# Encoder block on one core: where the opening builds the differences of its transposed input

## The chip, the cores and the metric

The kernel runs on one core of one Trainium2 chip. Five engines of the core run side by side, each with an instruction stream of its own that it works through in order: TensorE (PE in the profile; its weight loads are a row of their own, PEld), VectorE (DVE), ScalarE (ACT), GpSimd (POOL) and SyncE (SP), which here issues most DMAs. PE writes its products to PSUM, eight banks of 128 x 512 float32; DVE and ACT read them there. The metric is the device time of one execution in microseconds (us), as a median of runs.

## The reference: what is computed

A transformer-like block over 1024 tokens of width 1024, float32, one layer. The opening, which is all that this change touches, is the first two of these lines: the layer norm of the input, and the projection of its result by one matrix of 1024 x 11776.

```python
h = layer_norm(x, ln_in_g, ln_in_b)
proj = h @ w_in[l]
aq, ak, av, hq, hf_fwd, hf_bwd, hi, hg, ga, gh = jnp.split(proj, split_idx, axis=-1)
att = dilated_attention(aq, ak, av, slopes)
rec = hgrn2(hq, hf_fwd, hf_bwd, hi, hg, lower_bounds[:, l], hgrn_norm_g[l])
merged = jax.nn.sigmoid(ga) * (att @ w_att_up[l]) + jax.nn.sigmoid(gh) * (rec @ w_hgrn_up[l])
h = layer_norm(DEEPNORM_ALPHA * h + merged @ w_o[l], ln1_g[l], ln1_b[l])
gate, up = jnp.split(h @ w_ffn_in[l], 2, axis=-1)
h = layer_norm(DEEPNORM_ALPHA * h + (jax.nn.silu(gate) * up) @ w_ffn_out[l], ln2_g[l], ln2_b[l])
```

## The kernel before

**Products.** Every large matrix product is done by the Strassen-Winograd scheme: both factors are cut into 2 x 2 blocks, and seven block products replace eight. Each float32 block is further split into a high part (rounded to the type `float32r`, by ACT) and a low part (the rest, by DVE or POOL), and a block product sums high x high, high x low and low x high in PSUM (`mm3`, L270 to L272). A block product of 512 x 512 moving data takes 4 x 3 = 12 instructions of PE, called products below.

**The moving side.** `phase0` (L316) makes it from x. Token rows come in eight tiles `xt` of 128 x 1024. For each, `stats` (DVE, then three small steps on POOL) finds mean and inverse deviation, and `norm(tt, q)` normalises half q of tile tt (512 columns) on ACT. `turn` transposes 128 x 128 pieces on PE into PSUM banks (tag `sd`, four of them, shared with some block products). The four blocks of the transposed input are b11 and b21 (first and second 512 features of tiles 0 to 3), b12 and b22 (the same of tiles 4 to 7). The gain of the layer norm is a factor and its bias a summand per partition in this layout. From the blocks come t1 = b12 - b11, t2 = b22 - t1, t3 = b22 - b12 and t4 = b21 - t2, each in four pieces k of 128 features.

Helpers of `phase0`: `scaled` takes a bank times the gain to SBUF, on ACT or DVE; `less` takes a bank times the gain less another tile (DVE); `hi` makes a high part with the bias (ACT); `lo` makes the low part (DVE). Tiles that are needed only in the opening are lent the buffers of later forms (`lent`): w11 (b11 without its bias) lies in that of b22's high part, t1 in that of t3's, w22 (b22 without its bias) in that of t4's, z2 (t2 without its bias) in that of t4's low part. `forms(n)` gives a buffer its final use, which waits until what was lent is read. w21 is b21 without its bias; its buffers are named v in the profile.

Before, t3's difference is made in SBUF by POOL, z2 - w11 (L467), t4's too, w21 - z2 (L482); b22 is copied raw from its banks by ACT and split late, after t3.

**The stationary side.** `stream` (L615) is a generator; each `next` (by `run` in `phase0`) issues one block product. Its order is: product 1 (b11) for two units of two column groups each, product 2 (b21) for both, then products 6 (t2), 5 (t1), 7 (t3), 3 (b22), 4 (t4) of unit 0, then of unit 1, and so on over 23 units. Ahead of each, `sums` (L644) forms the sums of weight blocks and `prep` splits a weight block into `w_hi` (ACT, L212) and `w_lo` (POOL, L222) and issues the DMA that refills the block. `leave` evicts the banks into the outputs of the projection (DVE and ACT, L529 to L559, and L680) at high priority.

**Order.** The program's text gives priorities. At build a scheduler lays out each engine's stream from them by its own estimate of time; `ordered`, `left` and `behind` add order edges between two instructions. Loads of x and of weights are kept in program order on SP's queue (`queued`).

Of the kernel before, what the change touches and what calls it, by code (L numbers as in the profile page):

```python
# [10 lines left out]
F32 = mybir.dt.float32  # L11
F32R = mybir.dt.float32r
I32 = mybir.dt.int32
AF = mybir.ActivationFunctionType
# [65 lines left out]
class Block:  # L80
# [152 lines left out]
        self.issued[key] = ins.ins.name  # L233
        return ins

    gone = None

    def left(self, ins):
        self.gone = ins.ins.name
# [76 lines left out]
    def phase0(self, pool, work):  # L316
# [4 lines left out]
        def lent(tag):  # L321
            t = self.xp.tile([128, 4, HALF], F32, name=f"lent_{tag}", tag=tag, bufs=1)
            return [t[:, k, :] for k in range(4)]

        w11, t1, w22, z2 = (lent(z) for z in ("xb22hi", "xt3hi", "xt4hi", "xt4lo"))
        w21 = [self.half("v21") for _ in range(4)]

        strict = True

        def act(*args, **kw):  # L330
            ins = nc.scalar.activation(*args, **kw)
            return self.ordered("xact", ins) if strict else ins

        def dve(ins):
            return self.ordered("xdve", ins) if strict else ins
# [9 lines left out]
        def stats(tt):  # L345
            st = self.tiny.tile([128, 2, 6], F32, name="bn0", tag="bnst", bufs=3)
            for j in range(2):
                dve(nc.vector.bn_stats(st[:, j, :], xs[tt][:, HALF * j:HALF * (j + 1)]))
            mv = self.mv0[:, tt, :]
            dve(nc.vector.bn_aggr(mv[:, 0:2], st))  # L350
            nc.gpsimd.tensor_scalar(mv[:, 2:3], mv[:, 1:2], LN_EPS, None, op0=OP.add)
            nc.gpsimd.tensor_tensor(mv[:, 2:3], mv[:, 2:3], self.mhalf[:, 0:1], OP.pow)
            nc.gpsimd.tensor_scalar(mv[:, 3:4], mv[:, 0:1], mv[:, 2:3], -1.0, op0=OP.mult, op1=OP.mult)

        def norm(tt, q):
            x, mv = xs[tt][:, HALF * q:HALF * (q + 1)], self.mv0[:, tt, :]
            return act(x, x, AF.Identity, bias=mv[:, 3:4], scale=mv[:, 2:3])

        def turn(tt, q, ks=range(4)):
# [7 lines left out]
        def column(n, k):  # L367
            return self.col[n][:, k:k + 1]

        def scaled(w, k, q, on_act):  # L370

            g = column("gin", 4 * q + k)
            if on_act:
                act(w[k], banks[k], AF.Copy, scale=g)
            else:
                dve(nc.vector.tensor_scalar(w[k], banks[k], g, None, op0=OP.mult))

        def less(o, k, q, w):

            dve(nc.vector.scalar_tensor_tensor(o[k], banks[k], column("gin", 4 * q + k), w[k], op0=OP.mult,  # L380
                                               op1=OP.subtract))

        def hi(name, k, src, b=None):
            z = self.xb[name][0][:, k, :]
# [23 lines left out]
        for tt in range(4):  # L408
            norm(tt, 0)
            turn(tt, 0)  # L410
            if tt < 3:
                stats(tt + 1)
                norm(tt, 1)
        bias = [[column("bin", 4 * q + k) for k in range(4)] for q in range(2)]
        scaled(w11, 0, 0, True)
        scaled(w11, 1, 0, False)
        scaled(w11, 3, 0, False)
# [20 lines left out]
            self.left(lo("b21", k, w21, bias[1][k]))  # L438
        self.rest()
        strict = False  # L440
        for tt in range(4, 8):
            norm(tt, 0)
            if tt < 7:
                stats(tt + 1)
            norm(tt, 1)
        run(3)
        for k in (0, 2):
            for tt in range(4, 8):
                turn(tt, 0, (k, k + 1))
            for i in (k, k + 1):  # L450
                less(t1, i, 0, w11)
            run()
        for k in (0, 2):
            for tt in range(4, 8):
                turn(tt, 1, (k, k + 1))
            for i in (k, k + 1):
                less(z2, i, 1, t1)
            for i in (k, k + 1):
                h = hi("t2", i, z2, bias[1][i]), lo("t2", i, z2, bias[1][i])
                scaled(w22, i, 1, True)  # L460
            run()
        for k in range(4):
            self.behind(hi("t1", k, t1), h[0].ins.name)
            last = lo("t1", k, t1)
            self.behind(last, h[1].ins.name)
        for k in range(4):
            self.behind(nc.gpsimd.tensor_sub(w11[k], z2[k], w11[k]), last.ins.name)  # L467
        diff = self.tiny.tile([128, 4], F32, name="diff", tag="bnmv", bufs=3)
        nc.gpsimd.tensor_sub(diff, self.col["bin"][:, 4:8], self.col["bin"][:, 0:4])
        run(2)  # L470
        self.forms("t3")
        for k in range(4):
            hi("t3", k, w11, diff[:, k:k + 1])
            last = lo("t3", k, w11, diff[:, k:k + 1])
        run(2)
        self.forms("b22")
        for k in range(4):
            hi("b22", k, w22, bias[1][k])
            lo("b22", k, w22, bias[1][k])
        run()  # L480
        for k in range(4):
            self.behind(nc.gpsimd.tensor_sub(w21[k], w21[k], z2[k]), last.ins.name)  # L482
        self.forms("t4")
        for k in range(4):
            hi("t4", k, w21)
# [129 lines left out]
    def stream(self, tiles, pool):  # L615


        nc, tc = self.nc, self.tc
        self.cols = [c for c, _ in tiles]
        O = self.ORDER  # L620
        order = [(n, (p,)) for p in O[:2] for n in (0, 1)]
        order += [(n, O[2:] if n < 2 else O) for n in range(len(tiles) // 4)]
        seq = [(n, g, p) for n, part in order for p in part for g in range(2)]
        after = {6: "a11", 7: "a21", 3: "a12", 4: "a22"}
        A, first = [{}, {}], {}
        for g in range(2):
            A[g]["a11"] = self.block(0, g, "a11")
        yield
        for g in range(2):
            first[g, 1] = self.block(1, g, "a11", pool)  # L630
        for g in range(2):
            A[g]["a12"] = self.block(0, g, "a12")
        yield
        for b in ("a21", "a22"):
            for g in range(2):
                A[g][b] = self.block(0, g, b)
        yield
        state = [[{}, {}], [{}, {}]]
        ready = {}

        def early(n):
            return tc.high_priority(offset=self.evac_ahead if n > 1 else 0)

        def sums(i):  # L644
            if i >= len(seq):
                return
            n, g, p = seq[i]
            a = A[g]
            with early(n):
                if p == 6:  # L650
                    a["s1"] = self.blk.tile([128, 4, 128], F32, name="ws1", tag=f"s1{g}", bufs=1)
                    self.behind(nc.vector.tensor_add(a["s1"], a["a21"], a["a22"]))
                    nc.vector.tensor_sub(a["a11"], a["s1"], a["a11"])  # L653
                    nc.gpsimd.tensor_sub(a["a21"], a["a22"], a["a11"])  # L654
                    a["s3"], a["s2"] = a["a21"], a["a11"]
                elif p == 3:
                    self.behind(nc.vector.tensor_sub(a["a12"], a["a12"], a["s2"]))
                    a["s4"] = a["a12"]

        def prep(i):  # L660
            if i >= len(seq):
                return
            n, g, p = seq[i]
            if n == 1 and p == 2:
                first[g, 2] = self.block(1, g, "a12", pool)
            with early(n):
                ready[i] = self.granules()
                self.split(*ready[i], first[g, p] if n == 1 and p < 3 else A[g][self.PRODUCTS[p][0]],
                           key="w" if i < 4 else None)
            if p in after and 4 * n + 4 < len(tiles):  # L670
                A[g][after[p]] = self.block(n + 1, g, after[p])

        def bank(n, g, p):
            if (n, p) in ((0, 5), (0, 2), (1, 2)):
                return self.ps_sd()
            return self.ps_pj(2 * g + (n + (p == 1)) % 2)

        def keep(ps, tag):
            t = self.ws.tile([128, HALF], F32, name="wkeep", tag=tag, bufs=1)
            nc.scalar.copy(t, ps)  # L680
            return t

        for i in range(3):
            prep(i)
        yield
        for i, (n, g, p) in enumerate(seq):
            late = i + 5 < len(seq) and seq[i + 5][0::2] == (1, 6)
            if not late:
                sums(i + 5)
            prep(i + 3)  # L690
            if late:
                sums(i + 5)
            s = state[n % 2][g]
            if p in (1, 2) or p == 5 and n < 2:
                s[min(p, 2)] = bank(n, g, p)
            ps = s[1 if p in (1, 6, 7, 4) else 2]
            hi, lo = ready.pop(i)
            xhi, xlo = self.xb[self.PRODUCTS[p][1]]
            for k in range(4):
                self.mm3(ps, hi[:, k, :], lo[:, k, :], xhi[:, k, :], xlo[:, k, :], p in (1, 2, 5) and k == 0, k == 3,  # L700
                         skip_group_check=True)
            self.leave(tiles[4 * n + 2 * g:4 * n + 2 * g + 2], p, ps, s, keep,
                       f"k{5 if (n, p) == (1, 1) else 1}{g}", f"k5{g}")
            yield 4 * n + 2 * g + 2 if p == 4 else 0
# [1208 lines left out]
```

## Time and profile before

| | us |
|---|---|
| median of 3 runs | 2074.36 |
| lowest and highest | 2071.59, 2077.41 |
| profiled execution, its own time | 2071.3 |
| its span | 2069.5 |

| engine, whole span | busy us |
|---|---|
| PE | 2016.2 |
| DVE | 1325.4 |
| POOL | 1074.7 |
| ACT | 953.8 |

The profile lists instructions with start and duration, and groups of them. The idle time ahead of an instruction and the one that released it stand in brackets or behind the last bar. Names are those of the program's tiles: `sd` and `pj` are PSUM banks, `wa`, `wfirst` and `ws` weight blocks and their sums, `lent_...` the buffers lent in the opening, `vc` the columns of gains and biases, `evh` and `wkeep` evicted results. A matmul's duration overlaps that of the next. The granted clock is 1.00 at full speed and 0.50 at half.

### The profile page before, as it was taken

The numbers are of one execution on the slowest core, as the hardware profiler recorded it, in microseconds if no ns is written. First come the engines' busy times: TensorE is split into PE (matmuls) and PEld (weight loads), VectorE is DVE, ScalarE is ACT, GpSimd is POOL, SyncE is SP. The second block draws the span as 40 slices with busy tenths as digits, with TensorE's granted clock in tenths as the row PEclk, the third lists the DMA queues.
The fourth block names the chain that finished last, engine by engine and source line by source line (L and its number), as shares of the span: only waits on it lengthen the run. The fifth ranks groups of instructions, "written<-read, shape, count | busy, mean of one in ns | idle before, by whom it ended". The sixth has DMA issues, their size and how long they took to land. (4 is left out here: it accounts for less than half of the span.)

```text
span 2069.5 us, 30921 instructions
## 1 busy us (share of the span) xinstructions
PE 2016.2 (97%) x10974; PEld 1669.0 (81%) x10974; DVE 1325.4 (64%) x2017; ACT 953.8 (46%) x1968; POOL 1074.7 (52%) x919
## 2 busy tenths in 40 slices
PE   7899999999999999999999999999999999999998
PEld 5688888888887888888888888787888888888876
DVE  6966645884368744776343225547776776758777
ACT  6554455553655436454365432244433333334542
POOL 5766744776356653665536662344665665620012
PEclk9999999999999999999999999999999999999999
DMA  5443433435333452344524376444444443447423
GB/s 157 133 139 125 158 122 105 157 126 173 97 123 133 131 163 93 122 139 137 166 93 154 124 249 219 154 145 139 154 137 138 133 137 132 144 158 270 164 89 127
DMA packets 274844, 297.95 MB, mean 144 GB/s; under 512 B 14017, under 2 KB 207362, under 8 KB 274690
## 3 DMA queue, kind: packets, MB, share of 16 engines
q1 hardware_dynamic: 268384, 274.78, 41.0%
q10 hardware_dynamic: 6306, 21.20, 2.6%
q8 instruction: 86, 1.41, 0.3%
q14 instruction: 68, 0.56, 0.1%
HBM read 201.29 MB, written 94.63 MB: 143 GB/s over the span
## 5 line engine op out<-in xcount | busy, mean ns | idle before, releaser
L222 POOL TENSOR_TENSOR w_lo<-wa,w_hi 128x512 fp32r<-128x512 f32 x272 | 363.2, 1345 | 277.8 <-ACT w_hi L212 250.3
L212 ACT CAST w_hi<-wa 128x512 fp32r<-128x512 f32 x272 | 168.4, 620 | 251.0 <-PE pj L271 165.3
L222 POOL TENSOR_TENSOR w_lo<-wsum,w_hi 128x512 fp32r<-128x512 f32 x88 | 127.7, 1460 | 111.3 <-PE sd L272 60.7
L222 POOL TENSOR_TENSOR w_lo<-f_raw,w_hi 128x512 fp32r<-128x512 f32 x66 | 102.1, 1555 | 55.2 <-ACT w_hi L212 54.0
L208 POOL TENSOR_TENSOR mv<-mv,mhalf 128x1 f32<-128x1 f32 x16 | 10.8, 680 | 208.3 <-DVE mv L207 208.2
L212 ACT CAST w_hi<-wsum 128x512 fp32r<-128x512 f32 x88 | 54.7, 621 | 122.2 <-PE sd L271 118.7
L270 PE MATMUL pj<-xt1hi,w_hi 128*128 128x512 f32 x252 | 99.8, 396 | 3.6 <-DVE evh L531 1.9
L270 PE MATMUL pj<-xb22hi,w_hi 128*128 128x512 f32 x252 | 99.3, 394 | 0.0
L272 PE MATMUL pj<-xb22hi,w_lo 128*128 128x512 f32 x252 | 98.5, 392 | 0.4 <-POOL w_lo L222 0.3
L542 DVE TENSOR_TENSOR evh<-wkeep,pj 128x512 f32<-128x512 f32 x45 | 30.8, 684 | 106.4 <-PE pj L272 61.2
L271 PE MATMUL pj<-xb22lo,w_hi 128*128 128x512 f32 x252 | 98.5, 391 | 0.0
L272 PE MATMUL pj<-xt1hi,w_lo 128*128 128x512 f32 x252 | 98.5, 391 | 0.0
L271 PE MATMUL pj<-xt1lo,w_hi 128*128 128x512 f32 x252 | 98.3, 390 | 0.0
L212 ACT CAST gwsum<-a_raw 128x512 fp32r<-128x512 f32 (+1 forms) x78 | 47.7, 616 | 101.6 <-PE pj L271 47.2
L654 POOL TENSOR_TENSOR wa<-wa,wa 128x512 f32<-128x512 f32 x46 | 65.1, 1424 | 49.5 <-DVE wa L653 44.0
L680 ACT COPY wkeep<-pj 128x512 f32<-128x512 f32 x136 | 79.4, 584 | 21.6 <-DVE evh L558 11.9
L531 DVE TENSOR_TENSOR evh<-wkeep,pj 128x512 f32<-128x512 f32 x66 | 57.5, 879 | 44.5 <-PE pj L272 33.9
L222 POOL TENSOR_TENSOR w_lo<-ws,w_hi 128x512 fp32r<-128x512 f32 x46 | 63.2, 1378 | 43.1 <-ACT w_hi L212 42.9
L222 DVE TENSOR_TENSOR gwkeep<-a_raw,gwsum 128x512 fp32r<-128x512 f32 (+1 forms) x78 | 57.7, 739 | 42.0 <-ACT gwsum L212 39.1
L270 PE MATMUL pj<-xt4hi,w_hi 128*128 128x512 f32 x192 | 76.4, 398 | 3.5 <-DVE evh L531 2.4
L272 PE MATMUL pj<-xt2hi,w_lo 128*128 128x512 f32 x192 | 75.5, 394 | 3.7 <-POOL w_lo L222 3.7
L270 PE MATMUL pj<-xb11hi,w_hi 128*128 128x512 f32 x192 | 76.8, 402 | 1.3 <-DVE wkeep L556 1.3
(421 smaller groups left out, 6585.1 us busy)
## 6 DMA issues: line engine op xcount, KB each, us to landing
wa<-in_w_in_dram SPq DMA_DIRECT2D x184, 256.0 KB, 3.3
f_raw<-in_w_ffn_in_dram SPq DMA_DIRECT2D x44, 512.0 KB, 4.0
a_raw<-gd SPq DMA_DIRECT2D x30, 512.0 KB, 3.6
gd<-fc SPq DMA_DIRECT2D x44, 256.0 KB, 2.0
gd<-fs SPq DMA_DIRECT2D x33, 256.0 KB, 2.1
tg<-evh SPq DMA_DIRECT2D x32, 256.0 KB, 2.3
tg<-tg SPq DMA_DIRECT2D x16, 512.0 KB, 3.6
y<-ahs SPq DMA_DIRECT2D x16, 512.0 KB, 4.6
```

Of the source, the lines that this page charges most:

```text
L208: nc.gpsimd.tensor_tensor(mv[:, 2:3], mv[:, 2:3], self.mhalf[:, 0:1], OP.pow)
L212: ins = nc.scalar.copy(hi, src) if eng_hi == "act" else nc.vector.tensor_copy(hi, src)
L222: ins = e.tensor_sub(lo, src, hi.bitcast(F32))
L270: nc.tensor.matmul(ps, whi, xhi, start=first, stop=False, **kw)
L271: nc.tensor.matmul(ps, whi, xlo, start=False, stop=False, **kw)
L272: self.product = nc.tensor.matmul(ps, wlo, xhi, start=False, stop=last, **kw).ins.name
L531: self.left(nc.vector.tensor_tensor(o, self.order_src(add, g, kind), s, OP.add))
L542: self.left(nc.vector.tensor_add(t, add, ps))
L654: nc.gpsimd.tensor_sub(a["a21"], a["a22"], a["a11"])
L680: nc.scalar.copy(t, ps)
```

## The change

It has five parts, all in `phase0` and `sums`:

- the first halves of the last two row tiles (tt 6 and 7) are normalised on DVE, the other 14 halves stay on ACT; the statistics of tiles 5 to 7 come first, then all first halves of tiles 4 to 7, then all second halves;
- the raw b12 is kept: `scaled` on ACT writes w12 from the bank (four instructions), and once the bank of b22 is there, `less` on DVE turns it into t3's difference in place (four). POOL's four subtractions for t3 go;
- b22's parts are made while its banks are held: the high part by ACT from the bank, then the high part less the bias (hb) by ACT with a negated bias column (nbin, one small POOL instruction), then the low part by DVE as bank times gain less hb. The four raw copies and the later split of b22 go;
- t4's four differences move from POOL to DVE;
- the first weight sums (product 6, first group) are held back in `later` and issued behind the first two pieces of t1. The three products that follow t3's split are asked for in one go instead of two and one.

```diff
-        w11, t1, w22, z2 = (lent(z) for z in ("xb22hi", "xt3hi", "xt4hi", "xt4lo"))
+        w11, w12, t1, hb, z2 = (lent(z) for z in ("xb22hi", "xt4hi", "xt3hi", "xt3lo", "xt4lo"))
...
             x, mv = xs[tt][:, HALF * q:HALF * (q + 1)], self.mv0[:, tt, :]
+            if tt > 5 and q == 0:
+                return dve(nc.vector.tensor_scalar(x, x, mv[:, 2:3], mv[:, 3:4], op0=OP.mult, op1=OP.add))
             return act(x, x, AF.Identity, bias=mv[:, 3:4], scale=mv[:, 2:3])
...
+        nc.gpsimd.tensor_scalar(nbin, self.col["bin"][:, 4:8], -1.0, None, op0=OP.mult)
...
-        for tt in range(4, 8):
-            norm(tt, 0)
-            if tt < 7:
-                stats(tt + 1)
-            norm(tt, 1)
+        for tt in range(5, 8):
+            stats(tt)
+        for q in range(2):
+            for tt in range(4, 8):
+                norm(tt, q)
+        self.later = []
         run(3)
         for k in (0, 2):
             for tt in range(4, 8):
                 turn(tt, 0, (k, k + 1))
             for i in (k, k + 1):
-                less(t1, i, 0, w11)
+                scaled(w12, i, 0, True)
+                self.left(less(t1, i, 0, w11))
+            if k == 0:
+                for z in self.later:
+                    z()
+                self.later = None
             run()
+        self.forms("b22")
         for k in (0, 2):
             for tt in range(4, 8):
                 turn(tt, 1, (k, k + 1))
             for i in (k, k + 1):
                 less(z2, i, 1, t1)
             for i in (k, k + 1):
+                less(w12, i, 1, w12)
+                g, b, z = column("gin", 4 + i), bias[1][i], self.xb["b22"][0][:, i, :]
+                act(z, banks[i], AF.Identity, bias=b, scale=g)
+                act(hb[i], z.bitcast(F32), AF.Identity, bias=nbin[:, i:i + 1])
+                dve(nc.vector.scalar_tensor_tensor(self.xb["b22"][1][:, i, :], banks[i], g, hb[i], op0=OP.mult,
+                                                   op1=OP.subtract))
+            for i in (k, k + 1):
                 h = hi("t2", i, z2, bias[1][i]), lo("t2", i, z2, bias[1][i])
-                scaled(w22, i, 1, True)
             run()
...
-        for k in range(4):
-            self.behind(nc.gpsimd.tensor_sub(w11[k], z2[k], w11[k]), last.ins.name)
...
-            hi("t3", k, w11, diff[:, k:k + 1])
-            last = lo("t3", k, w11, diff[:, k:k + 1])
-        run(2)
-        self.forms("b22")
+            hi("t3", k, w12, diff[:, k:k + 1])
+            last = lo("t3", k, w12, diff[:, k:k + 1])
+        run(3)
         for k in range(4):
-            hi("b22", k, w22, bias[1][k])
-            lo("b22", k, w22, bias[1][k])
-        run()
-        for k in range(4):
-            self.behind(nc.gpsimd.tensor_sub(w21[k], w21[k], z2[k]), last.ins.name)
+            self.behind(nc.vector.tensor_sub(w21[k], w21[k], z2[k]), last.ins.name)
...
-        def sums(i):
+        def sums(i, again=False):
             if i >= len(seq):
                 return
             n, g, p = seq[i]
             a = A[g]
+            if n == 0 and p == 6 and self.later is not None and not again:
+                self.later.append(lambda: sums(i, True))
+                return
```

More of the change, by code (lines that the diff above doesn't have):

```diff
@@ L234, in ordered @@
         return ins
-    gone = None
+    gone = later = None
     def left(self, ins):
@@ L323, in lent @@
             return [t[:, k, :] for k in range(4)]
-        w11, t1, w22, z2 = (lent(z) for z in ("xb22hi", "xt3hi", "xt4hi", "xt4lo"))
+        w11, w12, t1, hb, z2 = (lent(z) for z in ("xb22hi", "xt4hi", "xt3hi", "xt3lo", "xt4lo"))
         w21 = [self.half("v21") for _ in range(4)]
         strict = True
+        nbin = self.tiny.tile([128, 4], F32, name="nbin", tag="nbin", bufs=1)
         def act(*args, **kw):
@@ L378, in less @@
         def less(o, k, q, w):
-            dve(nc.vector.scalar_tensor_tensor(o[k], banks[k], column("gin", 4 * q + k), w[k], op0=OP.mult,
-                                               op1=OP.subtract))
+            return dve(nc.vector.scalar_tensor_tensor(o[k], banks[k], column("gin", 4 * q + k), w[k], op0=OP.mult,
+                                                      op1=OP.subtract))
         def hi(name, k, src, b=None):
@@ L458, in phase0 @@
             for i in (k, k + 1):
+                less(w12, i, 1, w12)
[3 more added lines that the diff above has]
+                dve(nc.vector.scalar_tensor_tensor(self.xb["b22"][1][:, i, :], banks[i], g, hb[i], op0=OP.mult,
+                                                   op1=OP.subtract))
+            for i in (k, k + 1):
                 h = hi("t2", i, z2, bias[1][i]), lo("t2", i, z2, bias[1][i])
-                scaled(w22, i, 1, True)
             run()
```

## The prediction

> **What bounds the kernel now.** I read the page first, then the windows, then the order of time on each engine over the opening.
>
> ```profile
> span 2069.5 us, 30921 instructions
> PE 2016.2 (97%) x10974; PEld 1669.0 (81%) x10974; DVE 1325.4 (64%) x2017; ACT 953.8 (46%) x1968; POOL 1074.7 (52%) x919
> ```
> ```profile
> 0.00:100.00 100.00, 76.88 (x315) 58.51 (x316) 81.58 (x107) 60.20 (x101) 64.35 (x80) 0.95 0.47 147
> 100.00:500.00 400.00, 398.06 (x2524) 335.04 (x2523) 257.93 (x399) 203.00 (x472) 253.51 (x236) 1.00 0.42 136
> ```
>
> TensorE (PE) bounds the span. The windows (stretch, length, busy time of PE, weight loads, DVE, ACT, POOL, granted clock, DMA) put 23.1 us of its 53.3 us of idle into the first 100 us, and 1.9 us into the next 400. The change works only in those 100 us, so I ask what PE waits for there, in order of time:
>
> ```profile
> 34.59 0.55 PE L364 MATMUL sd<-tabs_sb,xt 128*128 128x128 f32 x3
> 37.16 1.15 PE L364 MATMUL sd<-tabs_sb,xt 128*128 128x128 f32 x7 [2.03 <-DVE evh L542]
> 39.13 0.79 PE L270 MATMUL sd<-xb21hi,w_hi 128*128 128x512 f32 x1 [0.82 <-DVE lent_xt3hi L380]
> 44.42 1.16 PE L364 MATMUL sd<-tabs_sb,xt 128*128 128x128 f32 x8
> 53.41 0.39 PE L272 MATMUL sd<-xb21hi,w_lo 128*128 128x512 f32 x1
> 57.26 0.39 PE L270 MATMUL sd<-xt1hi,w_hi 128*128 128x512 f32 x1
> 58.42 0.40 PE L271 MATMUL sd<-xt1lo,w_hi 128*128 128x512 f32 x1
> 61.34 0.51 PE L271 MATMUL sd<-xt1lo,w_hi 128*128 128x512 f32 x1 [2.33 <-DVE xt1lo L390]
> 65.25 0.63 PE L270 MATMUL pj<-xt3hi,w_hi 128*128 128x512 f32 x2
> 73.00 0.39 PE L272 MATMUL pj<-xt3hi,w_lo 128*128 128x512 f32 x1
> 80.15 0.50 PE L270 MATMUL pj<-xt4hi,w_hi 128*128 128x512 f32 x1 [0.82 <-ACT w_hi L212]
> 89.60 0.50 PE L272 MATMUL pj<-xt2hi,w_lo 128*128 128x512 f32 x1 [1.22 <-POOL w_lo L222]
> 96.98 0.50 PE L272 MATMUL pj<-xt2hi,w_lo 128*128 128x512 f32 x1 [2.52 <-POOL w_lo L222]
> ```
>
> The reader sees a start, a duration and, in brackets, idle time and its releaser. Products overlap, so their price is from start to start: five from 57.26 to 58.42 give 0.23 us at full speed. Four stretches fall short of that:
> - A, 34.59 to 44.42: 10 transposes (0.145 each by the row of eight) and 12 products need 4.2 us and take 9.8. Lost 5.6.
> - B, 58.42 to 65.25: nine products need 2.07 and take 6.83. Lost 4.8.
> - C, 73.00 to 80.15: fifteen products need 3.4 and take 7.15. Lost 3.7; the waits there are for b22's low part and a weight.
> - D, the two waits for weights of the second unit: 3.7.
>
> All four together are 17.8 us, the most that an opening without stalls could return. Part of A and B is clock:
>
> ```profile
> 41.26:44.67 3.41, 3.41 (x10) 2.52 (x10) 0.01 (x1) 0.40 (x1) 0.76 (x1) 0.50 0.00 0
> 61.73:65.14 3.41, 3.07 (x8) 1.97 (x7) 3.21 (x10) 1.47 (x3) 0.85 (x5) 0.50 0.89 263
> 58.32:61.73 3.41, 1.08 (x6) 0.53 (x5) 3.41 (x4) 2.30 (x5) 2.67 (x3) 1.00 0.41 121
> 92.45:95.86 3.41, 1.81 (x7) 0.86 (x5) 3.41 (x3) 1.23 (x3) 3.41 (x4) 1.00 0.87 258
> ```
>
> A stretch in which PE was busy 1.08 of 3.41 us is followed by 3.41 us at half clock; one with 1.81 is not. So a gap of 2.3 us can cost 1.7 us more. The Trainium skill (TensorE: Matmul & The Clock Gate, "Part 1: The HAM clock gate") asks for a whole idle window of about 3.4 us before the clock halves. By that rule a remaining gap under 3 us costs only itself; here the trace halved it after 2.33 us, and the trace decides.
>
> **The change part by part.**
>
> *Rows, norms and first weight sums (stretch A).* What stood ahead of t1:
>
> ```profile
> 31.74 0.27 POOL L353 TENSOR_SCALAR mv<-mv 128x1 f32<-128x1 f32 x1
> 32.86 0.75 DVE L391 SCALAR_TENSOR_TENSOR xb21lo<-v,vc,xb21hi 128x512 fp32r<-128x512 f32 x1 [1.89 <-ACT xb21hi L331]
> 33.53 2.38 DVE L652 TENSOR_TENSOR ws<-wa,wa 128x512 f32<-128x512 f32 x2
> 36.12 1.53 ACT L331 ACTIVATE xt<-xt,mv 128x512 f32<-128x512 f32 x2
> 38.34 2.71 DVE L380 SCALAR_TENSOR_TENSOR lent_xt3hi<-sd,vc,lent_xb22hi 128x512 f32<-128x512 f32 x4
> 44.66 0.69 DVE L556 TENSOR_TENSOR wkeep<-wkeep,sd 128x512 f32<-128x512 f32 x1 [3.60 <-PE sd L272]
> ```
>
> The page names the DVE eviction as releaser of the transposes at 37.16, but the last row's first half is normalised by ACT only at 36.12 to 36.9, so ACT was as late. Both go: that half moves to DVE, which was idle for 1.89 us, and its statistics are ready at 32.0; the weight sums (33.53) step behind the first two t1. A DVE normalise from SBUF has no row: at best it hides in the 1.89 us, at worst two cost 2 x 1.2 (the half of 2.38); I take 0.7 each, as for t1, hidden. ACT loses two of 0.77 and gains nothing ahead of that. Then t1's first two are done at about 35, PE's second b21 group starts near 36 instead of 39.13 and at full clock ends near 39 instead of 44.42: 5.5 us ahead. The weight sums land about 2 us later, under a product group whose own end was 44.42; if that cover fails they cost those 2 us.
>
> *More work ahead of t2.* The raw b12 is kept by ACT (four, as many as the b22 copies that go) and turned into t3's difference by DVE; b22's high part, a copy less the bias (ACT), and its low part (DVE) now come straight from the PSUM banks ahead of t2.
>
> ```profile
> L380 DVE SCALAR_TENSOR_TENSOR lent_xt4lo<-sd,vc,lent_xt3hi 128x512 f32<-128x512 f32 x4 | 2.8, 743 | 0.0
> L391 DVE SCALAR_TENSOR_TENSOR xb22lo<-lent_xt4hi,vc,xb22hi 128x512 fp32r<-128x512 f32 x4 | 5.9, 1530 | 0.0
> L390 DVE TENSOR_TENSOR xt1lo<-lent_xt3hi,xt1hi 128x512 fp32r<-128x512 f32 x4 | 5.8, 1490 | 0.0
> L467 POOL TENSOR_TENSOR lent_xb22hi<-lent_xt4lo,lent_xb22hi 128x512 f32<-128x512 f32 x4 | 6.4, 1634 | 0.0
> L482 POOL TENSOR_TENSOR v<-v,lent_xt4lo 128x512 f32<-128x512 f32 x4 | 5.5, 1405 | 0.0
> ```
> ```profile
> 52.13 3.49 DVE L391 SCALAR_TENSOR_TENSOR xt2lo<-lent_xt4lo,vc,xt2hi 128x512 fp32r<-128x512 f32 x2
> 55.54 1.77 DVE L390 TENSOR_TENSOR xt1lo<-lent_xt3hi,xt1hi 128x512 fp32r<-128x512 f32 x1
> 59.54 4.04 DVE L390 TENSOR_TENSOR xt1lo<-lent_xt3hi,xt1hi 128x512 fp32r<-128x512 f32 x3
> 70.73 1.27 DVE L1073 TENSOR_SCALAR gna<-lbm 128x16 f32<-128x16 f32 x1
> 82.60 0.68 DVE L390 TENSOR_TENSOR xt4lo<-v,xt4hi 128x512 fp32r<-128x512 f32 x1
> ```
>
> DVE's clean price is 0.7 a step (0.68 for the last t4 low part); from two SBUF operands it rises to 1.5 to 1.8 while POOL works, from PSUM it stays at 0.74. From 33.6 to the last t2 low part DVE has t1 2.7, four weight sums 2.7, five eviction steps 3.4, t2 2.8, the new t3 differences 2.8 and b22 low parts 2.8, t2 low parts 2.8: 20.0, so 53.6 clean. Before, 5.6 fewer ended at 55.6, because DVE stood idle for 3.6 us behind A and POOL's 6.4 us of t3 differences lay beside it. POOL's weight low parts remain, and the b22 low parts wait for two ACT steps each while their banks stay taken: between 0 (other DVE work fills it) and 4 x 2 x 0.77 = 6.2 us (nothing does, ACT's price from the row at 36.12); I take 1.5, near the lower end, because the next bank's t3 difference and the evictions stand ready. So t2 is whole at 55, only 0.6 us earlier. PE, 5.5 us ahead, ends b21 at 48 (53.64 before), does what it can of t2 and then waits: at the start of t1 it has about 1 us left of the 5.5.
>
> *t1 (stretch B).* POOL's 6.4 us are gone and t1's low parts follow at once: four of 0.7 to 1.5 end between 57.8 and 61, against 63.6. The 24 t1 products (24 x 0.23 = 5.5 us) end near 62; from 57.26, with B's 4.8, they ended at 67.5. Of B's 4.8 I count 4.0.
>
> *b22 and t3 (stretch C).* b22 is complete some 20 us before use and 5.9 us of contended DVE work has become 2.8. t3 needs only its splits. Of 3.7 I count 3.5, leaving the weight wait.
>
> *t4 on DVE.* Four differences: 4 x 0.68 clean, 4 x 1.5 contended, 2.7 to 6.0; I take 4. They queue behind t3's last low part; behind them stand t4's low parts and evictions. DVE's balance to the last t4 low part (83.3) is +2.8 (t3) +4 (t4) -3.1 (b22) -3.2 (the three steps from 52.13 paid 5.3 beside POOL's t3 work, 2.1 clean) -3.6 (idle before the eviction at 44.66) and -3 (three 16-column steps like the one at 70.73 paid some 1.1 too much beside POOL's t4 work): about 6 ahead, where PE is 8.5 ahead. The t4 products take 5.5 us, so the last low part may trail; I charge 1.0.
>
> *Weights of the second unit (stretch D).*
>
> ```profile
> 73.19 3.41 POOL L222 TENSOR_TENSOR w_lo<-wa,w_hi 128x512 fp32r<-128x512 f32 x2
> 80.01 1.02 SPq L249 DMA_DIRECT2D wa<-in_w_in_dram  x2
> ```
>
> POOL's 5.5 us of t4 work held the splits at 73.19, and the next weight loads went out only at 80.01. Without it they go earlier, but so does PE. No DMA is added or moved past another; the negated bias is one small POOL step (0.27, as the row at 31.74) long before its use. Between 0 and 3.7; I take 2.0.
>
> **Sum:** 1.0 + 4.0 + 3.5 - 1.0 + 2.0 = 9.5 us. The profiled execution took 2071.3 us (span 2069.5), 3.1 under the median 2074.36, so 2061.8 for it and **2065** as a median.
>
> **Rivals.**
> - *DVE sets t2, or the gap only moves to the weights of the second unit.* For it: DVE was busy 81.58 of the first 100 us already. If every step from SBUF pays POOL's price, t2 is whole at 59 to 60, the wait takes in a half clock (1.7), t1 ends where it did, and C alone is won: 3 us, 2071. If the second unit's weights come when they came, little is won: 2073. Against: C and A do not hang on t2.
> - *Slower: DVE as the bound through t4.* Its in-order queue takes 5.6 us more ahead of t2, waits for ACT in each b22 low part (6.2), and the t4 differences cost 6.0 with t4 low parts queued behind. If no contention vanishes and only b22's 3.1 and the idle 3.6 are won, that is 11.1 us: the last t4 low part at 94 and PE 8 to 11 us later than now, 2082 to 2085. It decides once the last t4 low part falls more than 6 us behind 83.3. Against: POOL's work beside DVE falls by 11.9 us, the two groups above.
> - *Better: t2 in time and D gone.* 3 us more at t2, 1.7 at D, and A's clock: 2059 or less.
>
> **How the numbers follow.** A measurement of this kernel tells about 0.3%, 6.2 us, from no change: 2068.1 and 2080.6. Forecast (2060 to 2068) 0.48; better 0.14; first rival 0.23; slower 0.15. Faster 0.62, same 0.23, slower 0.15. Low end 2055 (the better case with D's rest); high end 2079, which leaves out most of the slower case. What the build does to the order of the later 1,960 us can't be read from the trace; it is in the range, not in the sum. The forecast's own range is 2060 to 2069.
>
> **What would show it.** In the changed profile: no half clock near 41; the second b21 group from about 36; t3's differences as PSUM steps of 0.74 on DVE; a PE wait for t2's low parts near 51 to 55; t1 products ending near 62; no wait for b22; the last t4 low part near 77. It is wrong if t2's low parts end past 58, if b22's low parts each cost PE a bank wait, or if PE's place at 100 us is ahead and the span is not.

## The result and the profile after

| | us |
|---|---|
| before, median of 6 runs | 2074.55 (2071.59 to 2077.41) |
| after, median of 6 runs | 2086.18 (2082.96 to 2088.05) |
| ratio after / before | 1.0054, 95% interval 1.0042 to 1.0065 |
| profiled execution of after, its own time | 2083.3 |

The changed kernel is slower by 0.54%, 11.6 us. The forecast was 2065 and the high end of its range 2079. The top of the page of after:

```profile
span 2081.1 us, 30934 instructions
PE 2028.5 (97%) x10974; PEld 1665.9 (80%) x10974; DVE 1314.0 (63%) x2027; ACT 954.6 (46%) x1970; POOL 1069.2 (51%) x912
```

PE issues as many matmuls as before (10974) and is busy 12.3 us longer (2016.2 before). Its idle time is 52.6 us, against 53.3. So the loss isn't a wait: the same products take longer. The windows of after say where not to look and where to look (stretch, length, busy time and count of PE, weight loads, DVE, ACT, POOL, granted clock, DMA share, GB/s):

```profile
0.00:100.00 100.00, 79.26 (x347) 62.00 (x347) 81.06 (x119) 63.95 (x107) 64.66 (x78) 0.98 0.48 152
...
1500.00:1600.00 100.00, 100.00 (x431) 80.42 (x430) 69.67 (x67) 36.04 (x62) 60.49 (x41) 1.00 0.40 134
```

The stretch from 1500 us in before:

```profile
1500.00:1600.00 100.00, 100.00 (x443) 82.81 (x442) 72.74 (x69) 36.35 (x63) 61.54 (x43) 1.00 0.42 141
```

In the opening PE does more than before (347 matmuls in 100 us, 315 before). But at 1500 us, where the change has no line, it issues 431 in 100 us instead of 443, both times without idle time and at full clock. The same stretch in order of time (start, duration, engine, line, operation); before:

```profile
1500.15 0.39 PE L271 MATMUL sd<-xt3lo,w_hi 128*128 128x512 f32 x1
1500.38 0.39 PE L272 MATMUL sd<-xt3hi,w_lo 128*128 128x512 f32 x1
1500.61 0.39 PE L270 MATMUL sd<-xt3hi,w_hi 128*128 128x512 f32 x1
1500.83 0.39 PE L271 MATMUL sd<-xt3lo,w_hi 128*128 128x512 f32 x1
```

After:

```profile
1500.58 0.40 PE L270 MATMUL sd<-xt3hi,w_hi 128*128 128x512 f32 x1
1500.81 0.39 PE L271 MATMUL sd<-xt3lo,w_hi 128*128 128x512 f32 x1
1501.05 0.40 PE L272 MATMUL sd<-xt3hi,w_lo 128*128 128x512 f32 x1
1501.28 0.39 PE L270 MATMUL sd<-xt3hi,w_hi 128*128 128x512 f32 x1
```

From start to start the same products stand 0.227 us apart before and 0.233 after. The mean over 1500 such pairs is 226.67 ns before and 233.33 ns after. I number the matmuls of both profiled executions in order of their start and subtract the starts (after less before; the time in brackets is that of before):

| matmul | after less before, us |
|---|---|
| 250 (80.5 us) | -5.1 |
| 325 (102 us) | -7.2 |
| 400 (117 us) | -1.7 |
| 500 (140 us) | -3.0 |
| 7000 (1149 us) | -1.6 |
| 8500 (1493 us) | +1.8 |
| 9000 (1606 us) | +5.2 |
| 10000 (1833 us) | +11.8 |
| the last | +12.0 |

The opening itself wins 3.0 us in this pair of executions. Then the row stays between -1.3 and -4.4 for a thousand microseconds, and between 1149 and 1833 us 13.4 are lost, from matmul 8500 to 10000 at a steady rate: 10.0 us over 1500 products, which is 6.67 ns for each. These are the products of the feed-forward's first factor; those with `att` and `rec`, from 1188 to 1322 us, go at 233.3 ns too (226.7 before). The projection (228.0 ns in both kernels) keeps its distance, and so does the feed-forward's second product (226.9 ns before, 227.0 after) but for 132 of its 924 products.

### The profile page after: what moved, and what is told of

Its sections match the earlier page's. It is cut to its first block, busy times and chain, and to the rows that moved or that the text cites. A ratio compares the mean times of both kernels' runs of the same rounds, so it can differ in the third digit from the quotient of the medians.

```text
span 2081.1 us, 30934 instructions
## 1 busy us (share of the span) xinstructions
PE 2028.5 (97%) x10974; PEld 1665.9 (80%) x10974; DVE 1314.0 (63%) x2027; ACT 954.6 (46%) x1970; POOL 1069.2 (51%) x912
## 5 line engine op out<-in xcount | busy, mean ns | idle before, releaser
L222 POOL TENSOR_TENSOR w_lo<-wa,w_hi 128x512 fp32r<-128x512 f32 x272 | 370.0, 1369 | 272.5 <-ACT w_hi L212 259.9
L222 DVE TENSOR_TENSOR gwkeep<-a_raw,gwsum 128x512 fp32r<-128x512 f32 (+1 forms) x78 | 57.8, 741 | 41.0 <-ACT gwsum L212 38.1
L271 PE MATMUL pj<-xt2lo,w_hi 128*128 128x512 f32 x192 | 76.1, 397 | 3.1 <-DVE xt2lo L394 3.1
```

Of the source, the lines that this page charges most:

```text
L222: ins = e.tensor_sub(lo, src, hi.bitcast(F32))
L271: nc.tensor.matmul(ps, whi, xlo, start=False, stop=False, **kw)
```

## Experiments: what makes every product 6.7 ns longer

**What differs at 1500 us.** After matmul 504, PE's instructions stand in the same order in both kernels. What the change moved there is an address. `nbin`, the negated bias, is a new tile of 128 x 4 floats (`self.tiny.tile([128, 4], F32, ...)`, L329 of the changed kernel, a line that the diff above does not show), and the built program gives it 32 bytes of each partition ahead of everything that is allocated later on the left side of SBUF. Byte addresses within a partition in the two programs:

```
tile                              before    after
nbin                                   -     2240
att_hi (later xt1hi of the FFN)     2528     2560
xt1hi of the projection            69600    69600
w_hi (first buffer)               212960   212960
```

I write d for the address of the stationary block (the weight) less that of the moving block, modulo 256. Before, d is 0 everywhere; after, 224 (32 short of it) wherever the moving block lies on the left (2748 products), and still 0 in the projection and most of the last product, whose two factors lie on the right. Theory: d sets the distance of the products. Rivals: another order of the work, or the new steps themselves.

**Before, with the shift alone.** The unchanged kernel, with an unused tile of 16 bytes where `nbin` would stand.

```diff
         strict = True
+        self.pad(self.tiny, 16)
```

> The kernel before with nothing but a tile of 16 bytes per partition allocated (and set to zero by one small POOL instruction) where the changed kernel has its negated bias column. PLACE: products at 233.3 ns in the later phases, 2087 to 2092 us, about 1.007 of before. ORDER: 2074 to 2076 us, no change beyond 0.2%.

2086.29 us (6 runs), ratio 1.0069 (1.0056 to 1.0082). The window of this kernel:

```profile
1500.00:1600.00 100.00, 100.00 (x430) 80.30 (x429) 69.37 (x68) 35.90 (x62) 59.67 (x42) 1.00 0.40 132
```

All 10974 matmuls stand in the order of before, nothing else is changed but one small fill, and the whole loss is there: 14.3 us by the ratio (the medians differ by 12.3), mean distance 233.33 ns. Order and new steps are out as causes of it.

**After, with `nbin` where no tile moves.** Four unused columns of a constant tile hold it.

```diff
-        nbin = self.tiny.tile([128, 4], F32, name="nbin", tag="nbin", bufs=1)
+        nbin = self.mhalf[:, 4:8]
```

> The changed kernel with the negated bias column in four unused columns of a tile that is there already, so that no tile of the program moves against the kernel before. Theory PLACE, sharpened by the runs so far (start to start of products 226.7 ns where data and weights differ by a multiple of 128 bytes modulo 128, 228.9 at a difference of 64, 233.3 at 32): all dense phases at 226.7 ns. What is left is the opening's own worth. If the lead of 7 us that the changed kernel has at 100 us lasts to the end: 2066 to 2069 us. Rival POOL: the lead is given back between 95 and 140 us, where POOL works without a pause on weight low parts and the first recurrence unit, and only some 3 us last: 2069 to 2073 us.

2072.66 us (12 runs), ratio 0.9988 (0.9976 to 0.9999). Its window:

```profile
1500.00:1600.00 100.00, 100.00 (x443) 82.84 (x442) 72.00 (x68) 36.47 (x63) 62.18 (x42) 1.00 0.41 136
```

The distance is 226.67 ns again, and 13.5 us come back (2086.18 less 2072.66). So two numbers stand apart: the place costs some 14 us, and the opening as changed wins about 2.5 (0.12% of 2074, barely told from nothing).

**Which address matters.** Two kernels with d = 192, got in different ways: the block 64 bytes further with the weights unmoved, and the block 32 further with the weights 32 back.

```diff
-        nbin = self.tiny.tile([128, 4], F32, name="nbin", tag="nbin", bufs=1)
+        nbin = self.tiny.tile([128, 16], F32, name="nbin", tag="nbin", bufs=1)[:, 0:4]
```

> The changed kernel with one number altered: the negated bias column takes 64 bytes of each partition instead of 16, so that all tiles allocated after it on that side of SBUF lie at 32 modulo 64 bytes again, as before, instead of 0. Theory PLACE: the products of the later phases (start to start 226.7 ns before, 233.3 ns changed, from 1180 to 1320 us and from 1420 to 1850 us) are slower because their moving data lie elsewhere modulo 64. Then the 233.3 ns vanish and with them some 15 to 16 us: 2069 to 2072 us, about 0.998 of before. Rival ORDER: they are slower because the scheduler laid the later work out otherwise, or because of what PE met earlier. Then the time stays at 2085 to 2088 us, 1.0054 of before.

```diff
+        self.rpad = self.pool("rpad", "right")
+        self.pad(self.rpad.__enter__(), 32)
         self.wpool = self.pool("wp", "right")
```

> The changed kernel with 32 bytes more at the very end of the other side of SBUF: moving data and stationary weights of all phases lie at 0 modulo 64. PLACE in its first form (data at 0 are slow by themselves): as with the data alone at 0, or slower, 2095 to 2115 us. PLACE in its second form (data and weights in different halves of 64 bytes are slow): all products at 226.7 ns again, 2068 to 2073 us. ORDER: 2080 to 2092 us.

2077.57 us (12 runs), 1.0024 (1.0010 to 1.0037); and 2076.85 (10 runs), 1.0020 (1.0006 to 1.0034). Windows of the first and of the second:

```profile
1500.00:1600.00 100.00, 100.00 (x439) 82.05 (x438) 71.57 (x68) 36.95 (x64) 61.29 (x43) 1.00 0.41 135
```
```profile
1500.00:1600.00 100.00, 100.00 (x439) 82.05 (x438) 71.93 (x68) 35.66 (x62) 61.95 (x42) 1.00 0.40 135
```

Both have 439 matmuls and 228.9 ns. In the first the block lies 32 bytes off a multiple of 64 and in the second on one; only the difference is the same. But I had expected the first to be as quick as before, and 2.2 of the 6.7 ns are left: a step of 64 bytes doesn't restore the place. The second fits none of the three times that I had written down for it.

**The projection's turn.** After, with an unused tile of 32 bytes in the pool of weights. The weights' own tiles stay at 212960, and what is allocated behind them on the right moves by 32: the projection's blocks, and one factor of the last product.

```diff
         self.wp = self.wpool.__enter__()
+        self.pad(self.wp, 32)
```

> The changed kernel with 32 bytes more on the other side of SBUF, below the weights: the moving data of the projection phase (the first 1100 us) now lie at 0 modulo 64 too, the stationary weights stay at 32. PLACE: the projection's 3864 products also go at 233.3 ns where nothing else bounds them, up to 26 us more: 2095 to 2112 us. ORDER: within 0.3% of the changed kernel, 2080 to 2092 us.

2100.11 us (4 runs), 1.014 (1.012 to 1.016). The projection's distance goes from 228.0 to 233.2 ns (d is 32) and that of most of the last product from 226.9 to 233.3 (d is 224). The other 132 products of the last have d = 192 here, and their distance is 228.9: each group follows its own d within one execution.

**The step at which it returns.** Before again, with larger unused tiles at the same place, one time each (before beside them: 2075.07 as a median of 15 for 96 and 128 bytes, one time of 2077.63 for 256 and 512):

```diff
         strict = True
+        self.pad(self.tiny, 96)
```

The others have 128, 256 and 512 in place of 96.

> The same with 96 bytes more. If the law is that of odd halves (32 and 96 alike): 233.3 ns in the late phases, 2085 to 2092 us. If it grows and falls with the distance in another way: 226.7 to 233.3 ns, a value not seen yet.

> The kernel before with 128 bytes more ahead of the left-hand tiles. If a difference of 128 bytes between data and weights counts as none, the products of the late phases stay at 226.7 ns and the time at 2070 to 2078 us. If any shift slows them: 228.9 or 233.3 ns, 2077 to 2090 us.

> The kernel before with 256 bytes more ahead of the left-hand tiles. In the kernel before data and weights differ by a multiple of 512 bytes (one piece of stationary weights is 512 bytes per partition). If the law repeats every 512 bytes: still slow, 228.9 to 233.3 ns in the late phases and 2077 to 2092 us. If it repeats every 256: 226.7 ns and 2070 to 2078 us.

> The same with 512 bytes more. If the law repeats every 512 or every 256 bytes: 226.7 ns in the late phases and 2070 to 2078 us. If it does not repeat within 512 bytes: 228.9 or 233.3 ns and 2077 to 2092 us.

2090.3, 2086.66, 2071.31 and 2074.45 us. The windows with 128 and with 256 bytes:

```profile
1500.00:1600.00 100.00, 100.00 (x430) 80.46 (x429) 69.79 (x67) 35.57 (x61) 60.77 (x41) 1.00 0.40 132
```
```profile
1500.00:1600.00 100.00, 100.00 (x443) 82.81 (x442) 71.98 (x68) 36.46 (x63) 62.16 (x42) 1.00 0.41 136
```

128 bytes are as slow as 32, which ended my guess of a step of 128; with 256 and 512 the distance is that of before.

**The weights moved instead.** Before, with the weights 16 bytes into larger tiles (d is 16 and 144 in turn; in the last product, where these tiles are the moving side, 240 and 112, and 0 in 132 products).

```diff
-        return [p.tile([128, 4, 128], F32R, name=n, tag=n, bufs=bufs) for n in ("w_hi", "w_lo")]
+        return [p.tile([128, 544], F32R, name=n, tag=n, bufs=bufs)[:, 4:516].rearrange("p (k c) -> p k c", c=128) for n in ("w_hi", "w_lo")]
```

> The kernel before with the split weights 16 bytes further into buffers of 2176 instead of 2048 bytes, so that data and weights differ by 112 modulo 128 in all phases. If 226.7 ns, found at a difference of 0, is the best there is, the products take 228 to 236 ns and the time is 2080 to 2120 us. Rival: the smaller step finds a faster place, below 226.7 ns, and the time falls under 2070.

2101.52 us (one time), 26.5 above the median of before beside it (2075.07): all stages at 231.2 to 233.3 ns, but for the 132 products with d = 0, which go at 227.05. Together, in the stage at 1500 us unless another is named:

| d | start to start, ns | kernel |
|---|---|---|
| 0 | 226.67 | before; after with `nbin` elsewhere; 256 and 512 bytes |
| 192 | 228.89 | two ways |
| 224 | 233.33 | after; before with 16 bytes |
| 160, 128 | 233.33 | 96 and 128 bytes |
| 16 and 144 | 233.33 | weights moved |
| 32 | 233.20 | projection, right side moved |

## Experiments: what the opening itself is worth

All but the last start from after with `nbin` in the constant tile (the version of 2072.66 us), so that the place doesn't blur them.

**The first weight sums back in front.**

```diff
-        self.later = []
         run(3)
...
-            if k == 0:
-                for z in self.later:
-                    z()
-                self.later = None
```

> The same, but the first weight sums are not held back: they stand ahead of t1 again. If holding them back is what shortened the first stall, the second b21 group starts 2 to 3 us later than in the run with everything in its place (38 us) and the end is 0 to 3 us later. Rival: DVE was idle from 34.3 to 37.3 us in the changed kernel, waiting for PSUM banks that ACT reads first, and the sums fit into that: the second group starts within 0.5 us of it, t2's low parts come 1 to 2 us sooner, and the time is the same or up to 2 us shorter.

2069.21 us (10 runs), 0.9968 (0.9956 to 0.9981): 0.20% under the version that holds them back, with a half-width of 0.17% on that difference, so 4 us, within 0.6 to 7.7. This version beats both kernels of the case. The second b21 group starts 1.05 us earlier here (37.80 against 38.85). From matmul 140 to 160 the version that holds the sums back loses 5.7 us against before, in part at half clock, and this one 0.9, at full clock. PE's wait for t2 in the version that holds them back, and then here:

```profile
49.66 0.79 PE L271 MATMUL pj<-xt2lo,w_hi 128*128 128x512 f32 x1 [3.12 <-DVE xt2lo L394]
```
```profile
46.13 0.51 PE L271 MATMUL pj<-xt2lo,w_hi 128*128 128x512 f32 x1 [0.54 <-DVE xt2lo L394]
```

**t4's differences back on POOL.**

```diff
-            self.behind(nc.vector.tensor_sub(w21[k], w21[k], z2[k]), last.ins.name)
+            self.behind(nc.gpsimd.tensor_sub(w21[k], w21[k], z2[k]), last.ins.name)
```

> The run with everything in its place, but t4's four differences on POOL again. If POOL is what takes the lead back, its 5.5 us more delay the weight low parts behind them and PE is 2 to 5 us later at 100 us; the end is 1 to 4 us later. Rival: DVE was the tighter one there, then PE is no later and the end the same within 1 us.

2077.33 us (12 runs), 1.0002 (0.9989 to 1.0014): 0.14% above the version with them on DVE, half-width 0.17%. Not told apart. In this pair of traces PE is 2.2 us later at matmul 325, but 1.8 of that stand at matmul 120 already, ahead of all work for t4.

**No half rows on DVE.**

```diff
-            if tt > 5 and q == 0:
-                return dve(nc.vector.tensor_scalar(x, x, mv[:, 2:3], mv[:, 3:4], op0=OP.mult, op1=OP.add))
```

> The run with everything in its place, but the first halves of the last two row tiles normalised on ACT (in the new order, first halves before second ones). ACT has 1.5 us more ahead of the last transposes of b12: the second b21 group starts 0.5 to 1.5 us later, and the end is 0 to 2 us later.

2072.92 us (12 runs), 0.9999 (0.9987 to 1.0011): 0.11% above, half-width 0.17%. Not told apart either. The second b21 group starts 2.1 us later (40.96 against 38.85) and at half clock, more than I had expected, but at matmul 160, behind the first waits for t2, this version is level again (0.4 us ahead).

**Rows and t4 alone, t3 and b22 as before.** Before, with the new order of rows, the two half rows on DVE and t4 on DVE:

```diff
+            if tt > 5 and q == 0:
+                return dve(nc.vector.tensor_scalar(x, x, mv[:, 2:3], mv[:, 3:4], op0=OP.mult, op1=OP.add))
...
-            self.behind(nc.gpsimd.tensor_sub(w21[k], w21[k], z2[k]), last.ins.name)
+            self.behind(nc.vector.tensor_sub(w21[k], w21[k], z2[k]), last.ins.name)
```

> The kernel before with the new order of norms, two half rows on DVE and t4's differences on DVE; t3's differences stay on POOL in SBUF, b22 is copied raw and split late, and the weight sums are in front. No tile moves. It differs from the run with the sums in front (2069.2 us, 0.9968 of before) by the PSUM part alone. If making t3's difference and b22's low part from PSUM carries the gain (no wait for b22, 3 to 4 us, and no POOL work beside t1's low parts), this one ends at 2072 to 2075 us. Rival: the norms carry it, and it ends within 1.5 us of 2069.

2073.86 us (11 runs), 0.9998 (0.9987 to 1.0009). The version with the sums in front has this and the parts from PSUM (t3's difference and b22, with the three products behind them asked for in one go), and stands 0.30% lower, half-width 0.17%: by these times the parts are worth about 6 us (2.7 to 9.7), the rest of the opening nothing that these runs can tell. The two were timed in different sessions, each against before, and their traces do not show such a gain in the opening: of the profiled executions (2069.32 us here, 2067.96 with the parts) the second is 2.1 us ahead at matmul 250, but 0.6 behind at 400 and 1.4 ahead at the end. So the 6 us are a difference of times whose cause is not shown.

## Why the prediction was wrong, step by step

**The step that failed** is "the negated bias is one small POOL step (0.27 ...) long before its use", costed at nothing, with "the order of the later 1,960 us ... in the range, not in the sum". The instruction is free; its tile is not. 32 bytes moved every later tile of the left side; 2748 products got another d, and the loss, some 14 us against a forecast gain of 9.5, is the price of some 2100 of them. I thought of the order of the later work, which did not change, and not of its addresses. A hint stood in the kernel: L99 allocates a pad of 32 bytes (`CST_PAD`, L75) that holds no data, and I passed over it. The sign of the slower rival came true by another mechanism: t4 on DVE didn't bound anything.

The rest of the error, some 7 us, is in the opening: 9.5 forecast, 2.5 measured once the place is restored. Counted by matmuls in the pair of executions, after is 1.8 us behind before at the start of t1 (forecast: 1.0 ahead), 1.2 ahead at the end of t1 (5.0), 5.1 ahead behind b22 (8.5), still 5.1 in t4 (7.5) and 1.7 at matmul 400 (9.5). So the terms for t2 and for stretch D failed, and t1's in part. PE in after (start, duration, idle time and its releaser):

```profile
36.30 0.66 PE L367 MATMUL sd<-tabs_sb,xt 128*128 128x128 f32 x4 [0.78 <-DVE evh L552]
38.18 0.47 PE L270 MATMUL sd<-xb21hi,w_hi 128*128 128x512 f32 x1 [1.23 <-DVE lent_xt3hi L383]
...
41.87 0.49 PE L270 MATMUL sd<-xb21hi,w_hi 128*128 128x512 f32 x1
...
48.98 0.50 PE L271 MATMUL pj<-xt2lo,w_hi 128*128 128x512 f32 x1 [3.11 <-DVE xt2lo L394]
...
62.13 0.50 PE L272 MATMUL sd<-xt1hi,w_lo 128*128 128x512 f32 x1 [1.35 <-POOL w_lo L222]
...
66.13 0.39 PE L272 MATMUL sd<-xt1hi,w_lo 128*128 128x512 f32 x1
...
77.24 0.39 PE L270 MATMUL pj<-xt4hi,w_hi 128*128 128x512 f32 x1
```

The group that starts at 41.87 here starts in before at:

```profile
45.33 0.48 PE L270 MATMUL sd<-xb21hi,w_hi 128*128 128x512 f32 x1
```

DVE, and then ACT, in after:

```profile
33.15 0.55 DVE L359 TENSOR_SCALAR xt<-xt,mv 128x512 f32<-128x512 f32 x1 [0.43 <-POOL mv L354]
...
35.55 0.69 DVE L552 TENSOR_TENSOR evh<-wkeep,sd 128x512 f32<-128x512 f32 x1 [1.20 <-PE sd L272]
37.28 1.41 DVE L383 SCALAR_TENSOR_TENSOR lent_xt3hi<-sd,vc,lent_xb22hi 128x512 f32<-128x512 f32 x2 [1.04 <-ACT lent_xt4hi L332]
38.61 1.28 DVE L665 TENSOR_TENSOR ws<-wa,wa 128x512 f32<-128x512 f32 x2
...
47.18 1.75 DVE L394 SCALAR_TENSOR_TENSOR xt2lo<-lent_xt4lo,vc,xt2hi 128x512 fp32r<-128x512 f32 x1
...
55.98 0.75 DVE L394 SCALAR_TENSOR_TENSOR xt2lo<-lent_xt4lo,vc,xt2hi 128x512 fp32r<-128x512 f32 x1
...
59.05 1.90 DVE L393 TENSOR_TENSOR xt1lo<-lent_xt3hi,xt1hi 128x512 fp32r<-128x512 f32 x3
...
72.65 1.62 DVE L393 TENSOR_TENSOR xt4lo<-v,xt4hi 128x512 fp32r<-128x512 f32 x1
```
```profile
36.56 1.83 ACT L332 ACTIVATE lent_xt4hi<-sd,vc 128x512 f32<-128x512 f32 x3
...
57.50 0.61 ACT L212 CAST w_hi<-ws 128x512 fp32r<-128x512 f32 x1
```

And POOL:

```profile
46.66 1.72 POOL L222 TENSOR_TENSOR w_lo<-ws,w_hi 128x512 fp32r<-128x512 f32 x1
58.18 3.89 POOL L222 TENSOR_TENSOR w_lo<-ws,w_hi 128x512 fp32r<-128x512 f32 x1 [9.80 <-ACT w_hi L212]
62.03 1.30 POOL L222 TENSOR_TENSOR w_lo<-wa,w_hi 128x512 fp32r<-128x512 f32 x1
```

- **Stretch A, half right.** The half rows took 0.55 us (0.7 forecast), and the second b21 group runs at full clock; but it starts at 38.18, not near 36, and the next at 41.87, 3.5 us ahead of before's 45.33 (5.5 forecast). I wrote that ACT "gains nothing ahead of that". It gains the copies of w12 at 36.56, from the same banks as t1, and DVE's t1 waits 1.04 us for them. DVE stands idle 1.20 and 1.04 us, room that the weight sums had filled; held back, they stand ahead of t2 instead.
- **t2, wrong.** Its low part at 47.18 comes late and takes 1.75 us beside a weight split on POOL (a later one takes 0.75), PE waits 3.11 us, and the clock halves. With the sums in front the wait is 0.54 and the clock stays full there, which fits the 4 us. The last t2 low part ends at 56.73 (55 forecast, 55.61 before). The windows on both sides of the clock's step:

```profile
46.93:50.34 3.41, 1.36 (x6) 1.14 (x7) 3.41 (x5) 2.11 (x5) 1.45 (x1) 1.00 0.20 77
50.34:53.75 3.41, 3.41 (x11) 2.53 (x10) 3.41 (x6) 2.47 (x4) 0.00 (x0) 0.50 0.03 13
```

- **t1 (stretch B), wrong in its size.** Its low parts end at 60.94, inside the 57.8 to 61 forecast. Its products end at 66.5, not 62. PE waits 1.35 us for a low part of weights. ACT made its high part only at 57.50, behind t1's and b22's in its queue; POOL stood idle 9.80 us for that and then took 3.89 beside DVE's steps. I charged the new steps to DVE alone, and not to ACT's queue. The queue alone doesn't make the wait, though: at the 1.30 of the next split, POOL would have been done at 59.5 (an estimate from these rows), before PE ran out of work at 60.8. (All this is read from the trace, not tried.) Counted by matmuls the stretch won 3.0 us of the 4.0 forecast; most of its lateness came in with t2.
- **b22 and t3 (stretch C), right.** No product waits for b22. From matmul 225 to 250 the lead grows from 1.2 to 5.1 us, 3.9 against 3.5 forecast. The groups of DVE steps of after, 30 to 78 us (count | busy, mean ns | idle ahead), show the prices:

```profile
L474 DVE SCALAR_TENSOR_TENSOR xb22lo<-sd,vc,lent_xt3lo 128x512 fp32r<-128x512 f32 x4 | 3.0, 746 | 0.0
...
L383 DVE SCALAR_TENSOR_TENSOR lent_xt4hi<-sd,vc,lent_xt4hi 128x512 f32<-128x512 f32 x4 | 3.0, 738 | 0.0
...
L393 DVE TENSOR_TENSOR xt1lo<-lent_xt3hi,xt1hi 128x512 fp32r<-128x512 f32 x4 | 2.6, 691 | 0.0
L492 DVE TENSOR_TENSOR v<-v,lent_xt4lo 128x512 f32<-128x512 f32 x4 | 2.5, 684 | 0.0
```

  b22's low parts cost 746 ns instead of 1530 and t1's 691 instead of 1490. The Trainium skill (SBUF — State Buffer, "Who interferes with whom") says that a DVE instruction with two SBUF inputs contends with a GpSimd instruction that reads SBUF. The rows agree, and show that either side can pay: t1's low parts cost 799 ns less than beside POOL's t3 differences, but three of the four ran beside a weight split on POOL again (from 59.05), and there it was the split that took 3.89 us instead of 1.30.
- **t4, better than forecast.** The differences took 2.5 us (4 forecast), the last low part ended at 74.26 (77 forecast), no PE wait follows; the 1.0 charged was not paid.
- **Stretch D, wrong.** I counted 2.0 won. The lead of 7.2 us at matmul 325 shrinks to 1.7 at 400. After, and then before:

```profile
88.00:97.00 9.00, 8.11 (x36) 6.35 (x35) 9.00 (x7) 2.67 (x6) 9.00 (x9) 1.00 0.69 229
95.00:118.00 23.00, 19.86 (x88) 15.59 (x87) 22.91 (x20) 10.67 (x20) 19.11 (x17) 1.00 0.42 133
```
```profile
88.00:97.00 9.00, 5.06 (x21) 3.25 (x19) 9.00 (x8) 5.05 (x9) 7.77 (x6) 1.00 0.75 246
95.00:118.00 23.00, 21.02 (x101) 17.57 (x102) 23.00 (x17) 8.78 (x15) 21.93 (x21) 1.00 0.40 125
```

  Before lost 3.9 us of PE in the nine from 88 and 2.0 in the 23 from 95; after loses 0.9 and then 3.1. PE comes earlier and the weights don't. The same 5.5 us are given back in the versions of 2072.66 and 2069.21 us, whatever their lead: the first rival's second half, a gap that only moves. That POOL's work for the first recurrence unit holds the weights there is read from the trace and wasn't tried.

## What to carry to other kernels

A change that adds or resizes a tile changes the addresses of those allocated after it: compare the start-to-start time of the same matmuls in a stage that the change doesn't touch before explaining a loss by its logic, and price a new tile by what it moves. If that time has changed, put the new tile into spare columns or pad it until the difference of the two operands' addresses is as it was, and judge the change then. And when an engine gives work away or takes some, count what it gains in its whole queue: ACT's new copies held t1 and, by the trace, a weight split, though ACT was busy under half of the span.

## What the hardware showed that I had not expected

A product of 512 columns with a weight load of its own takes 226.67 ns from start to start when the addresses of its moving and its stationary block differ by a multiple of 256 bytes, 228.89 at a difference of 192 and 233.33 at 224, 160 and 128 (2.9% more). Neither address alone decides. What in the chip does this no run here shows, and differences of 64 and 96 weren't tried. The Trainium skill (SBUF — State Buffer, "Who interferes with whom") says "PE and ACT never wait on anyone"; these 6.67 ns don't show who or what is waited for, only that the place of two operands changes PE's rate at a granted clock of 1.00 and without idle time, which that sentence doesn't lead one to expect.
